# Seven-product pairs in four more projections of a hybrid decoder block, and a last column that keeps half of its weights

## The chip, the cores and the metric

The kernel runs on one core of one Trainium2 chip. The metric is the device time in microseconds (us) of one execution. Engines are named as in the profile: PE is TensorE's matmul, PEld its weight load, DVE is VectorE, ACT is ScalarE, POOL is GpSimd, SP is SyncE, which issues the weight DMAs.

## The reference

One layer of a decoder block over 256 tokens with a model width of 2048, in float32:

```python
u = rmsnorm(h, g_mix)
q, k, v, z, xbc, dt, g_a, g_s = split(u @ w_in)
out_a = sliding_window_attention(q, k, v) @ w_attn_br
y = rmsnorm(ssd(conv(xbc), dt) * silu(z), g_ssd)
out_s = y @ w_ssd_br
h = h + (sigmoid(g_a) * out_a + sigmoid(g_s) * out_s) @ w_o
f = rmsnorm(h, g_ffn)
h = h + (silu(f @ w_gate) * (f @ w_up)) @ w_down          # hidden width 5632
h = h + sigmoid(rmsnorm(h, g_ple) @ w_ple_gate) * (p @ w_ple_proj)
return rmsnorm(h, g_final)
```

## The kernel before

**Numbers in two parts.** Each float32 operand of a projection is split into a high part (a cast, on ACT) and a low part (the operand less its high part, on DVE). A product is three matmuls into one accumulator: high by high, high by low, low by high. The activations lie with features on partitions (uT, yT, mergedT, hT, actT, h2T: four k-tiles of 128 features by 256 tokens each, in both parts) and are the stationary operand, 128 tokens at a time; the weights are the moving operand, 512 columns at a time.

**`nblock`** computes one block of 512 columns for both token tiles. It loads two k-tiles of weights per step (512 KB, tile `wr`, a ring of 4), casts them (`wh`, a ring of 4), takes the low parts (`wl`, a ring of 3), issues 12 matmuls, and then runs one piece of side work. It uses two of the four PSUM tiles of one pool; transposes use the other pool.

**`wide_block`** (only in the hidden stage before) computes two blocks of 512 columns, those of `w_gate` and `w_up`, into four accumulators, and swaps the two PSUM pools each time. It goes by pairs of k-tiles. An ordinary pair is two loads of 512 KB and 24 matmuls. A seven-product pair takes a 2 x 2 block product (two token tiles, two k-tiles, two column blocks) in seven products, 21 matmuls, instead of eight: DVE makes four sums of weights (`tr`, split into `th` and `tl`), the activations come as four combinations (`forms`, made by `token_forms`), and four shared sums collect in the other pool's four PSUM tiles. After the last such pair the shared sums are combined into a large tile `mid` (`parts`). At the end of the block each accumulator is combined with its part. The hidden stage has such pairs at `hforms` 2 and 5, eight pairs to a block.

**Order.** The code is written in program order, and a scheduler orders the instructions of each engine from that order and from what each waits for, ahead of time; on the chip each engine takes its instructions in that order. `side` is a queue of pieces of work (transposes, normalization sums), one of which is run after each load's matmuls; `drain` runs what is left. `queue_flip` queues the two `transpose_pair`s by which 512 finished columns become features on partitions.

**Stages around the change**, with their times in the trace: the attention projection ends at about 500 us. Then come four columns, in turn the second gate (w_in at `GSO`, with uT) and the SSD projection (with yT), to 677 us; four columns of the output projection (with mergedT), to 769; and three thirds of the hidden width (4, 4 and 3 column blocks of `hidden`, each third followed by its part of the down projection over four columns, with actT), from 769 to 1490. Last comes the gate of the embedding: for each column `projected` and the gate product (with h2T). The weights of its last column are loaded and split ahead, two k-tiles a time (`load_last`), twice in each of the down columns 1 and 2 of the last third and of gate columns 1 and 2; the last column then runs from SBUF, token tile 0 first, then two halves of token tile 1, each followed by its finish. Large tiles (8 KB to a partition) share one pool of 17 buffers.

Of the kernel before, what the change touches and what calls it, by code (L numbers as in the profile page):

```python
# [11 lines left out]
F32 = mybir.dt.float32  # L12
# [49 lines left out]
def block_kernel(ctx: ExitStack, tc: tile.TileContext, x, x_t, p_t, positions, vecs, rows, g_final,  # L62
# [81 lines left out]
    def transpose_pair(src, col0, dst, j0, gains=None, form=None):  # L144

        ps = aux_tile().rearrange("p (j t) -> p j t", j=2)
        for j in range(2):
            for t in range(NT):
                c = col0 + j * P
                nc.tensor.transpose(out=ps[:, j, t * P:(t + 1) * P], in_=src[t][:, c:c + P],  # L150
                                    identity=ident)
        split_to(dst, j0, ps, gains)
        if form is not None:
            token_forms(ps, form, gains)
# [96 lines left out]
    def token_forms(src, dst, gains=None):  # L251


        sc = roll("fsc").rearrange("p (j t) -> p j t", j=2)
        for j in range(2):
            nc.scalar.activation(out=sc[:, j], in_=src[:, j], func=AF.Copy,
                                 scale=1.0 if gains is None else gains[j])
        fm = roll("fm").rearrange("p (f t) -> p f t", f=4)
        a11, a21, a12, a22 = sc[:, 0, :P], sc[:, 0, P:], sc[:, 1, :P], sc[:, 1, P:]
        for o, x, y, op in ((fm[:, 0], a22, a21, ALU.subtract), (fm[:, 1], fm[:, 0], a11, ALU.add),  # L260
                            (fm[:, 2], a12, fm[:, 1], ALU.subtract),
                            (fm[:, 3], a11, a21, ALU.subtract)):
            nc.vector.tensor_tensor(out=o, in0=x, in1=y, op=op)
        nc.scalar.copy(out=dst[:, :, 0], in_=fm)
        nc.vector.tensor_tensor(out=dst[:, :, 1], in0=fm, in1=dst[:, :, 0].bitcast(F32),
                                op=ALU.subtract)

    def wide_block(halves, lhs, nk, forms, pumps=1):
# [19 lines left out]
        for kp in range(np_):  # L288
# [56 lines left out]
        return [x.tile for x in sums], parts  # L345
# [277 lines left out]

    def hslice(g):
        return slice(g * HPG, (g + 1) * HPG)
# [37 lines left out]
    def queue_xs(g, src):  # L663
# [69 lines left out]
        def flip(i):  # L733
            def run():
                xd = mix[g, "xd"]
                transpose_pair([xd[:, t, 1] for t in range(NT)], i * 2 * P, yT[g], 2 * i,
                               [vcol(V_GSSD, 4 * g + 2 * i + j) for j in range(2)])
            return run
# [175 lines left out]
    mergedT = None  # L914
# [9 lines left out]
    drain(heads)  # L924
    r2 = const.tile([P, NT], F32, name="r2")
# [8 lines left out]
    mergedT = feat_tiles(4, "mergedT")  # L934

    def queue_flip(src, dst, j, gbase=None, forms={}):
        for i in range(2):
            def run(i=i):
                gains = None
# [5 lines left out]
    for j in range(4):  # L945
        accs = nblock(w_in, GSO + j * NB, lhs_u, KD)
        gs = [roll("gs") for _ in range(NT)]
        for t in range(NT):
            nc.scalar.activation(out=gs[t], in_=accs[0][t], func=AF.Sigmoid,
                                 scale=r1[:, t:t + 1])  # L950
        accs = nblock(w_ssd_br, j * NB, lambda k: stat(yT, k), KD)
        for t in range(NT):
            nc.vector.scalar_tensor_tensor(out=gs[t], in0=accs[0][t], scalar=r2[:, t:t + 1],
                                           in1=gs[t], op0=ALU.mult, op1=ALU.mult)
            nc.vector.tensor_tensor(out=merged[t][:, cols(j)], in0=merged[t][:, cols(j)],
                                    in1=gs[t], op=ALU.add)
        queue_flip(merged, mergedT, j)
# [6 lines left out]
    hT = feat_tiles(4, "hT")  # L964
    hforms = big([P, 2, 4, 2, P], F32R, name="hforms")
    hforms = {kp: hforms[:, i] for i, kp in enumerate((2, 5))}
# [6 lines left out]

    ssq3 = mean_parts(4, EPS, "ssq3")
    for j in range(4):
        accs = nblock(w_o, j * NB, lambda k: stat(mergedT, k), KD)
        for t in range(NT):
            nc.vector.tensor_tensor(out=h[t][:, cols(j)], in0=accs[0][t], in1=h[t][:, cols(j)],
                                    op=ALU.add)
        queue_flip(h, hT, j, V_GFFN, hforms)  # L980
        side.append(lambda j=j: square_sum(j, ssq3))
# [5 lines left out]
    def hidden(j, dst):  # L987
# [3 lines left out]
        for i, (o, op) in enumerate(((act[0], ALU.add), (parts[1], ALU.subtract),  # L991
                                     (act[1], ALU.add), (parts[3], ALU.subtract))):
            nc.vector.tensor_tensor(out=o, in0=sums[i], in1=parts[i], op=op)
# [5 lines left out]
        for i in range(2):  # L999
            side.append(lambda i=i: transpose_pair(act, i * 2 * P, dst, 2 * i))  # L1000

    last_h, last_l = [], []

    def load_last(c):


        if c % 2 == 0:
            last_h.append(big([P, 4, NB], F32R, name="last_h"))
            last_l.append(big([P, 4, NB], F32R, name="last_l"))
        wr = wraw_p.tile([P, 2, NB], F32, name="wr", tag="wr")  # L1010
        nc.sync.dma_start(out=wr, in_=w_ple_gate[c * 2 * P:(c + 1) * 2 * P, 3 * NB:].rearrange(
            "(k p) n -> p k n", p=P))
        ks = slice(2 * (c % 2), 2 * (c % 2) + 2)
        nc.scalar.copy(out=last_h[c // 2][:, ks], in_=wr)
        nc.vector.tensor_tensor(out=last_l[c // 2][:, ks], in0=wr,
                                in1=last_h[c // 2][:, ks].bitcast(F32), op=ALU.subtract)

    steps = deque(range(KD // 2))

    def run_ahead(chunks):  # L1020
        def run(c):
            if c in chunks and steps:
                load_last(steps.popleft())
        return run

    ssq4 = mean_parts(4, EPS, "ssq4")
    h2T = pT = gfin = None
    thirds = ((0, 4), (4, 8), (8, FFN // NB))
    for j0, j1 in thirds:
        last = j1 == FFN // NB  # L1030
        actT = []
        for j in range(j0, j1):
            actT.append(big([P, 2, 4, SEQ], F32R, name="actT"))
            hidden(j, actT[-1])
        drain()
        if last:
            h2T = feat_tiles(4, "h2T")
# [6 lines left out]
        for j in range(4):  # L1044
            accs = nblock(w_down[j0 * NB:j1 * NB], j * NB, lambda k, a=actT: stat(a, k),
                          4 * (j1 - j0), before=run_ahead((1, 3)) if last and j in (1, 2) else None)
            for t in range(NT):
                nc.vector.tensor_tensor(out=h[t][:, cols(j)], in0=accs[0][t],
                                        in1=h[t][:, cols(j)], op=ALU.add)
            if last:  # L1050
                queue_flip(h, h2T, j, V_GPLE)
                side.append(lambda j=j: square_sum(j, ssq4))
    drain()
    r4 = const.tile([P, NT], F32, name="r4")
# [4 lines left out]
    r5 = const.tile([P, NT], F32, name="r5")  # L1059
    def mix_in(t, ps, pp, c0, n):  # L1060
# [28 lines left out]
    def projected(j):  # L1089
        accs = nblock(w_ple_proj, j * NB, lambda k: stat(pT, k), PLE // P, tile_of=aux_tile)  # L1090
# [4 lines left out]

    nc.vector.memset(ssq5[:, :, 4:5], 0.0)
# [9 lines left out]
    for t in range(NT):  # L1106
        ts = slice(t * P, (t + 1) * P)
        for i, (s0, sn) in enumerate(((0, NB),) if t == 0 else ((0, NB // 2), (NB // 2, NB // 2))):
            o = acc_tile()[:, :sn]
            for k in range(KD):  # L1110
                hi, lo = stat(h2T, k)
                wh, wl = last_h[k // 4][:, k % 4], last_l[k // 4][:, k % 4]
                cs = slice(s0, s0 + sn)
                nc.tensor.matmul(o, hi[:, ts], wh[:, cs], start=(k == 0), stop=False)
                nc.tensor.matmul(o, hi[:, ts], wl[:, cs], start=False, stop=False)
                nc.tensor.matmul(o, lo[:, ts], wh[:, cs], start=False, stop=(k == KD - 1))
            mix_in(t, o, pp[t][:, cs], 3 * NB + s0, sn)
            square_in(t, 3 * NB + s0, sn, 3 + i)
            if s0 + sn < NB:
                gain_in(t, 3 * NB + s0, sn)  # L1120
        rsqrt_mean(ssq5[:, t:t + 1], r5[:, t:t + 1])
        gain_in(t, 3 * NB + s0, sn)
        finish(t)
# [57 lines left out]
```

## Time and profile before

| | us |
|---|---|
| median of 3 runs | 1599.76 |
| lowest, highest | 1598.59, 1599.88 |
| profiled execution, its time | 1600.46 |
| its span | 1598.8 |
| PE busy | 1584.0 (99%) |
| DVE busy | 1060.2 (66%) |
| ACT busy | 806.6 (50%) |

The span is that of the profiled execution, from the first to the last instruction; its time is 1.7 us longer than the span. Busy times of matmuls are of pipelined instructions: the mean of one 512-column matmul is about 390 ns long, and the next starts before it ends, so their pace is read from the starts.

### The profile page before, as it was taken

What the parts mean: (1) busy time and instruction counts of PE and PEld (TensorE: products, weight loads), DVE (VectorE), ACT (ScalarE), POOL (GpSimd) and SP (SyncE); (2) the same over time, 40 slices, a digit from 0 to 9 for tenths busy, and PEclk for the clock granted to TensorE, in tenths of its full rate; (3) what the DMA queues carried; (4) which work ended last, traced back from release to release, by engine and by line L of the source; (5) the groups of instructions that cost most, each with busy time, mean ns of one, the idle gap of its engine ahead of it and who ended that gap; (6) DMA issues with size and microseconds to landing.
All of it is one profiled execution on the core that took longest, in us unless ns stands there. A gap on an engine that the chain in (4) does not pass through costs nothing.

```text
span 1598.8 us, 19873 instructions
## 1 busy us (share of the span) xinstructions
PE 1584.0 (99%) x7348; PEld 1312.3 (82%) x7348; DVE 1060.2 (66%) x1274; ACT 806.6 (50%) x1020; POOL 131.6 (8%) x136
## 2 busy tenths in 40 slices
PE   9999999999999999999999999999999999999997
PEld 7988888888888888888888888888888888887886
DVE  7676767666655555456778775577775577776673
ACT  6654665555643444445554543445544344546552
POOL 1014224143210000000000000000000000000000
PEclk9999999999999999999999999999999999999999
DMA  8566435555657666655666656666665566756661
GB/s 267 172 193 186 143 105 158 158 160 157 178 185 218 190 190 185 197 184 185 185 192 203 194 189 197 187 204 194 194 196 188 193 187 204 225 194 223 198 211 53
DMA packets 152562, 296.63 MB, mean 186 GB/s; under 512 B 9537, under 2 KB 9665, under 8 KB 152081
## 3 DMA queue, kind: packets, MB, share of 16 engines
q1 hardware_dynamic: 151168, 290.76, 58.9%
q0 software_dynamic: 576, 3.47, 0.7%
q8 instruction: 57, 0.93, 0.2%
q10 hardware_dynamic: 720, 1.14, 0.2%
q14 instruction: 41, 0.33, 0.1%
HBM read 293.23 MB, written 2.10 MB: 185 GB/s over the span
## 4 chain that ended last, share of the span: by engine, by line
PE 94%; DMA 2%; ACT 1%; DVE 1%; issue 1%; POOL 0%; POOLq 0%; ACTq 0%; DVEq 0%; SPq 0%
PE acc L204 17%; PE acc L206 17%; PE acc L205 17%; PE aux L248 15%; PE acc L248 14%; PE aux L204 2%; PE aux L205 2%; PE aux L206 2%; PE aux L150 1%; DMA wr<-in_w_down_dram 1%; PE aux L709 1%; DVE wl L195 1%; PE aux L886 1%; PE acc L233 1%; PE aux L233 0%
## 5 line engine op out<-in xcount | busy, mean ns | idle before, releaser
L195 DVE TENSOR_TENSOR wl<-wr,wh 128x1024 fp32r<-128x1024 f32 (+1 forms) x356 | 452.3, 1274 | 324.3 <-PE acc L205 253.8
L193 ACT CAST wh<-wr 128x1024 fp32r<-128x1024 f32 (+1 forms) x356 | 367.6, 1035 | 439.7 <-PE acc L206 343.8
L204 PE MATMUL acc<-wh,uT 128*128 128x512 f32 (+1 forms) x640 | 250.6, 392 | 0.6 <-ACT cb L438 0.6
L206 PE MATMUL acc<-wh,uT 128*128 128x512 f32 (+1 forms) x640 | 243.9, 381 | 0.0
L205 PE MATMUL acc<-wl,uT 128*128 128x512 f32 (+1 forms) x640 | 243.6, 381 | 0.0
L298 DVE TENSOR_TENSOR wl<-wr,wh 128x1024 fp32r<-128x1024 f32 x132 | 159.4, 1221 | 61.8 <-issue 31.8
L248 PE MATMUL aux<-wh,hT 128*128 128x512 f32 x620 | 199.5, 391 | 0.0
L296 ACT CAST wh<-wr 128x1024 fp32r<-128x1024 f32 x132 | 138.6, 1054 | 115.9 <-PE aux L248 43.6
L248 PE MATMUL acc<-wh,hT 128*128 128x512 f32 x524 | 170.7, 392 | 0.0
L204 PEld LDWEIGHTS acc<-wh,uT 128*128 128x128 f32 x640 | 120.3, 188 | 22.8 <-issue 1.4
L206 PEld LDWEIGHTS acc<-wh,uT 128*128 128x128 f32 x640 | 120.1, 188 | 22.9
L205 PEld LDWEIGHTS acc<-wl,uT 128*128 128x128 f32 x640 | 120.4, 188 | 22.5 <-issue 1.0
L248 PEld LDWEIGHTS aux<-wh,hT 128*128 128x128 f32 x620 | 116.4, 188 | 24.0
L248 PE MATMUL aux<-wl,hT 128*128 128x512 f32 x310 | 120.7, 389 | 0.0
L248 PEld LDWEIGHTS acc<-wh,hT 128*128 128x128 f32 x524 | 98.4, 188 | 20.1
L248 PE MATMUL acc<-wl,hT 128*128 128x512 f32 x262 | 102.0, 389 | 0.0
L204 PE MATMUL acc<-wh,actT 128*128 128x512 f32 x256 | 99.8, 390 | 0.0
L206 PE MATMUL acc<-wh,actT 128*128 128x512 f32 x256 | 99.8, 390 | 0.0
L205 PE MATMUL acc<-wl,actT 128*128 128x512 f32 x256 | 99.6, 389 | 0.0
L324 ACT CAST wh<-wr 128x1024 fp32r<-128x1024 f32 (+1 forms) x44 | 36.9, 838 | 86.4 <-PE acc L248 43.1
L248 PEld LDWEIGHTS aux<-wl,hT 128*128 128x128 f32 x310 | 58.2, 188 | 11.7
L325 DVE TENSOR_TENSOR tl<-tr,th 128x2048 fp32r<-128x2048 f32 x22 | 50.4, 2290 | 11.6 <-ACT th L324 11.6
(344 smaller groups left out, 2572.8 us busy)
## 6 DMA issues: line engine op xcount, KB each, us to landing
wr<-in_w_in_dram SPq DMA_DIRECT2D x144, 512.0 KB, 3.6
wr<-in_w_gate_dram SPq DMA_DIRECT2D x88, 512.0 KB, 3.7
wr<-in_w_up_dram SPq DMA_DIRECT2D x88, 512.0 KB, 3.8
wr<-in_w_down_dram SPq DMA_DIRECT2D x88, 512.0 KB, 3.6
wr<-in_w_ssd_br_dram SPq DMA_DIRECT2D x32, 512.0 KB, 3.7
wr<-in_w_o_dram SPq DMA_DIRECT2D x32, 512.0 KB, 4.3
wr<-in_w_ple_gate_dram SPq DMA_DIRECT2D x32, 512.0 KB, 4.5
wr<-in_w_in_dram SPq DMA_DIRECT2D x32, 256.0 KB, 4.0
```

What stands on the lines that cost most here:

```text
L150: nc.tensor.transpose(out=ps[:, j, t * P:(t + 1) * P], in_=src[t][:, c:c + P], identity=ident)
L193: nc.scalar.copy(out=wh, in_=wr)
L195: nc.vector.tensor_tensor(out=wl, in0=wr, in1=wh.bitcast(F32), op=ALU.subtract)
L204: nc.tensor.matmul(o, hi[:, ts], wh[:, kk, cs], start=(k == 0), stop=False)
L205: nc.tensor.matmul(o, hi[:, ts], wl[:, kk, cs], start=False, stop=False)
L206: nc.tensor.matmul(o, lo[:, ts], wh[:, kk, cs], start=False, stop=(k == nk - 1))
L233: nc.tensor.matmul(o, hi[:, ts], wh[:, i], start=(k == 0), stop=False)
L248: nc.tensor.matmul(self.tile, a, b, start=self.first, stop=self.left == 0)
L296: nc.scalar.copy(out=wh, in_=wr)
L298: nc.vector.tensor_tensor(out=wl, in0=wr, in1=wh.bitcast(F32), op=ALU.subtract)
L324: nc.scalar.copy(out=xh, in_=x)
L325: nc.vector.tensor_tensor(out=xl, in0=x, in1=xh.bitcast(F32), op=ALU.subtract)
```

## The change

Four projections besides gate and up now go by `wide_block`, two column blocks of one weight matrix at a time (`column_pair`): the second gate with seven-product pairs 2 and 5 of eight (`uforms`, made from uT during the attention projection), the SSD projection with pair 4 (`yforms`), the output projection with pair 4 (`mforms`), and the down projection with pairs 2 and 5 of eight in the first two thirds and 3 of six in the last (`aforms`, made when the hidden columns are transposed). All of the second gate is computed ahead of the SSD projection, and its two wide blocks of gates are kept. Each accumulator is combined with its part by `settle` or, where it is added to h, by `add_settled`, two instructions. The large tiles of transposed activations are allocated when they are first written. The last column of the embedding's gate keeps only the second half of its k-tiles ahead (four loads, two of them in gate column 2 and two in the last column itself); the first half is loaded, split and used step by step for the three output pieces together, and then the kept half is run piece by piece, each followed by its finish.

```diff
-    def token_forms(src, dst, gains=None):
+    def scaled(ps, gains=None):
         sc = roll("fsc").rearrange("p (j t) -> p j t", j=2)
         for j in range(2):
-            nc.scalar.activation(out=sc[:, j], in_=src[:, j], func=AF.Copy,
+            nc.scalar.activation(out=sc[:, j], in_=ps[:, j], func=AF.Copy,
                                  scale=1.0 if gains is None else gains[j])
+        return sc
+
+    def joined(tiles, kp):
+        ks = slice(2 * (kp % 2), 2 * (kp % 2) + 2)
+        sc = roll("fsc").rearrange("p (j t) -> p j t", j=2)
+        src = tiles[kp // 2].bitcast(F32)
+        nc.vector.tensor_tensor(out=sc, in0=src[:, 0, ks], in1=src[:, 1, ks], op=ALU.add)
+        return sc
+
+    def token_forms(sc, dst):
...
+    def settle(i, sums, parts, out=None):
+        nc.vector.tensor_tensor(out=parts[i] if out is None else out, in0=sums[i], in1=parts[i],
+                                op=ALU.subtract if i % 2 else ALU.add)
+
+    def add_settled(i, dst, sums, parts):
+        nc.vector.tensor_tensor(out=dst, in0=dst, in1=parts[i],
+                                op=ALU.subtract if i % 2 else ALU.add)
+        nc.vector.tensor_tensor(out=dst, in0=sums[i], in1=dst, op=ALU.add)
...
+    YPAIRS, yforms = (4,), {}
...
+    UPAIRS = (2, 5)
...
+    side.extend(u_forms(kp) for kp in UPAIRS)
...
-    mergedT = feat_tiles(4, "mergedT")
+    mergedT = []
...
-    for j in range(4):
-        accs = nblock(w_in, GSO + j * NB, lhs_u, KD)
-        gs = [roll("gs") for _ in range(NT)]
...
-        accs = nblock(w_ssd_br, j * NB, lambda k: stat(yT, k), KD)
...
-        queue_flip(merged, mergedT, j)
+    gates = []
+    for jj in range(2):
+        sums, parts = wide_block(column_pair(w_in, GSO, jj), lhs_u, KD, uforms)
+        for i in range(4):
+            settle(i, sums, parts)
+            nc.scalar.activation(out=parts[i], in_=parts[i], func=AF.Sigmoid,
+                                 scale=r1[:, i // 2:i // 2 + 1])
+        gates.append(parts)
+    mforms = form_tiles((4,), "mforms")
+    for jj in range(2):
+        sums, parts = wide_block(column_pair(w_ssd_br, 0, jj), lambda k: stat(yT, k), KD, yforms)
+        for i in range(4):
+            t, c = i // 2, cols(2 * jj + i % 2)
+            settle(i, sums, parts)
+            nc.vector.scalar_tensor_tensor(out=parts[i], in0=parts[i], scalar=r2[:, t:t + 1],
+                                           in1=gates[jj][i], op0=ALU.mult, op1=ALU.mult)
+            nc.vector.tensor_tensor(out=merged[t][:, c], in0=merged[t][:, c], in1=parts[i],
+                                    op=ALU.add)
+        for q in range(2):
+            queue_flip(merged, mergedT, 2 * jj + q, None, mforms)
...
-        accs = nblock(w_o, j * NB, lambda k: stat(mergedT, k), KD)
...
+        add_to_h(jj, *wide_block(column_pair(w_o, 0, jj), lambda k: stat(mergedT, k), KD, mforms))
...
-    thirds = ((0, 4), (4, 8), (8, FFN // NB))
+    thirds = ((0, 4, (2, 5)), (4, 8, (2, 5)), (8, FFN // NB, (3,)))
...
-            accs = nblock(w_down[j0 * NB:j1 * NB], j * NB, lambda k, a=actT: stat(a, k),
-                          4 * (j1 - j0), before=run_ahead((1, 3)) if last and j in (1, 2) else None)
...
+            add_to_h(jj, *wide_block(column_pair(w_down[j0 * NB:j1 * NB], 0, jj),
+                                     lambda k, a=actT: stat(a, k), 4 * (j1 - j0), aforms))
...
-                      before=run_ahead((1, 4)) if j else None)
+                      before=run_ahead((3, 6)) if j == 2 else None)
...
+    ahead = run_ahead((0, 2))
+    for c in range(KD // 4):
+        ahead(c)
+        wr = wraw_p.tile([P, 2, NB], F32, name="wr", tag="wr")
+        nc.sync.dma_start(out=wr, in_=w_ple_gate[2 * c * P:2 * (c + 1) * P, 3 * NB:].rearrange(
+            "(k p) n -> p k n", p=P))
...
+        for kk in range(2):
+            for piece in range(3):
+                step(piece, 2 * c + kk, wh[:, kk], wl[:, kk])
+    for piece, (t, c0, n) in enumerate(pieces):
+        for i in range(KD // 2):
+            kh, kl = kept[i // 4]
+            step(piece, KD // 2 + i, kh[:, i % 4], kl[:, i % 4])
+        mix_in(t, outs[piece], pp[t][:, c0:c0 + n], 3 * NB + c0, n)
...
```

## Rows read from the trace of the kernel before

**Rows 1.** The page: span, and each engine's busy us, share of the span and instructions.

```profile
span 1598.8 us, 19873 instructions
...
PE 1584.0 (99%) x7348; PEld 1312.3 (82%) x7348; DVE 1060.2 (66%) x1274; ACT 806.6 (50%) x1020; POOL 131.6 (8%) x136
```

**Rows 2.** Windows by stage: us, busy us of each engine, granted clock, DMA share, GB/s.

```profile
547.00:591.50 44.50, 44.50 (x203) 36.85 (x201) 23.52 (x23) 19.10 (x20) 0.00 (x0) 1.00 0.62 189
...
812.00:855.50 43.50, 43.50 (x196) 35.60 (x195) 34.88 (x40) 23.20 (x25) 0.00 (x0) 1.00 0.64 194
1419.50:1489.70 70.20, 69.44 (x321) 56.95 (x320) 46.48 (x54) 39.06 (x56) 0.00 (x0) 1.00 0.64 210
1516.00:1541.00 25.00, 25.00 (x112) 20.71 (x111) 18.45 (x20) 15.42 (x20) 0.00 (x0) 1.00 0.73 236
1566.90:1590.00 23.10, 22.82 (x146) 20.66 (x145) 8.08 (x15) 5.25 (x12) 0.92 (x1) 1.00 0.13 46
```

**Rows 3.** The chain of waits in order of time: start us, length us, what.

```profile
547.01 0.44 PE aux L150 x4
...
591.48 0.44 PE aux L150 x4
...
703.23 0.44 PE aux L150 x4
...
725.94 0.44 PE aux L150 x4
...
812.08 2.72 PE acc L248 x12
...
843.92 11.56 PE acc L248 x51
855.48 2.72 PE aux L248 x12
```

**Rows 4.** Groups of DVE, first third of hidden blocks: count, busy us, mean ns.

```profile
L298 DVE TENSOR_TENSOR wl<-wr,wh 128x1024 fp32r<-128x1024 f32 x46 | 55.4, 1221 | 21.4 <-issue 11.9 <-PE aux L248 7.3 <-PE acc L248 2.2
...
L325 DVE TENSOR_TENSOR tl<-tr,th 128x2048 fp32r<-128x2048 f32 x8 | 18.3, 2290 | 3.5 <-ACT th L324 3.5
...
L316 DVE TENSOR_TENSOR tr<-wr 128x512 f32<-128x512 f32 x16 | 10.6, 686 | 0.5 <-DMA wr<-in_w_up_dram 0.5
...
L325 DVE TENSOR_TENSOR wl<-wr,wh 128x512 fp32r<-128x512 f32 x8 | 5.5, 689 | 1.9 <-PE aux L248 1.1 <-PE acc L248 0.7
L343 DVE TENSOR_TENSOR mid<-mid,aux 128x512 f32<-128x512 f32 x8 | 5.3, 684 | 0.1
...
L996 DVE SCALAR_TENSOR_TENSOR act<-mid,r,act 128x512 f32<-128x512 f32 x6 | 4.2, 745 | 0.0
```

**Rows 5.** Groups of DVE, output projection and start of the hidden stage.

```profile
L978 DVE TENSOR_TENSOR h<-acc,h 128x512 f32<-128x512 f32 x8 | 5.5, 688 | 3.9 <-PE acc L206 3.9
...
L265 DVE TENSOR_TENSOR hforms<-fm,hforms 128x512 fp32r<-128x512 f32 x2 | 1.4, 687 | 0.0
...
L263 DVE TENSOR_TENSOR fm<-fsc 128x128 f32<-128x128 f32 x4 | 1.0, 285 | 0.0
```

**Rows 6.** Timeline of DVE at the end of a hidden block, which is at 855.48.

```profile
852.12 0.69 DVE L993 TENSOR_TENSOR act<-acc,mid 128x512 f32<-128x512 f32 x1 [0.98 <-PE acc L248]
852.73 1.22 DVE L298 TENSOR_TENSOR wl<-wr,wh 128x1024 fp32r<-128x1024 f32 x1
...
855.45 1.22 DVE L298 TENSOR_TENSOR wl<-wr,wh 128x1024 fp32r<-128x1024 f32 x1
```

**Rows 7.** Waits of the weight loads, first third of hidden blocks.

```profile
PEld aux L248 <- DVE tl L325: 0.7, 2, 0.4
...
PEld acc L248 <- DVE tl L325: 0.4, 1, 0.4
```

**Rows 8.** The chain of waits at the end, token tile 0.

```profile
1578.24 0.70 ACT gt L1064
...
1581.41 0.92 POOL r L176
```

More of the change, by code (lines that the diff above doesn't have):

```diff
@@ L153, in transpose_pair @@
         if form is not None:
[L154 removed]
+            token_forms(scaled(ps, gains), form)
     def feat_tiles(n, name):
@@ L345, in wide_block, with form_tiles, column_pair @@
         return [x.tile for x in sums], parts
+    def settle(i, sums, parts, out=None):
[5 more added lines that the diff above has]
+        nc.vector.tensor_tensor(out=dst, in0=sums[i], in1=dst, op=ALU.add)
+    def form_tiles(pairs, name):
+        tile = big([P, 2, 4, 2, P], F32R, name=name)
+        return {kp: tile[:, i] for i, kp in enumerate(pairs)}
+    def column_pair(w, col0, jj):
+        return tuple((w, col0 + (2 * jj + q) * NB) for q in range(2))
     warm = roll("warm")
@@ L924, in block_kernel, with u_forms, run @@
     drain(heads)
+    UPAIRS = (2, 5)
+    uforms = {}
+    def u_forms(kp):
+        def run():
+            if kp == UPAIRS[0]:
+                uforms.update(form_tiles(UPAIRS, "uforms"))
+            token_forms(joined(uT, kp), uforms[kp])
+        return run
+    side.extend(u_forms(kp) for kp in UPAIRS)
     r2 = const.tile([P, NT], F32, name="r2")
@@ L972, in square_sum, with add_to_h @@
                                  accum_out=ssq[:, t, j:j + 1])
+    def add_to_h(jj, sums, parts):
+        for i in range(4):
+            add_settled(i, h[i // 2][:, cols(2 * jj + i % 2)], sums, parts)
     ssq3 = mean_parts(4, EPS, "ssq3")
-    for j in range(4):
-        accs = nblock(w_o, j * NB, lambda k: stat(mergedT, k), KD)
[L977 to L981, printed above, removed]
+    for jj in range(2):
+        add_to_h(jj, *wide_block(column_pair(w_o, 0, jj), lambda k: stat(mergedT, k), KD, mforms))
+        for q in range(2):
+            queue_flip(h, hT, 2 * jj + q, V_GFFN, hforms)
+            side.append(lambda j=2 * jj + q: square_sum(j, ssq3))
     drain()
@@ L984, in block_kernel, with hidden @@
     rsqrt_mean(ssq3, r3)
-    def hidden(j, dst):
+    def hidden(j, dst, kp0, forms):
         sums, parts = wide_block(((w_gate, j * NB), (w_up, j * NB)), lambda k: stat(hT, k), KD,
@@ L990, in hidden @@
         act = [roll("act") for _ in range(NT)]
-        for i, (o, op) in enumerate(((act[0], ALU.add), (parts[1], ALU.subtract),
-                                     (act[1], ALU.add), (parts[3], ALU.subtract))):
-            nc.vector.tensor_tensor(out=o, in0=sums[i], in1=parts[i], op=op)
+        for i in range(4):
+            settle(i, sums, parts, None if i % 2 else act[i // 2])
         for t in range(NT):
@@ L999, in hidden @@
         for i in range(2):
[L1000 to L1024, printed above, removed]
+            side.append(lambda i=i: transpose_pair(act, i * 2 * P, dst, 2 * i, None,
+                                                   forms.get(kp0 + i)))
     ssq4 = mean_parts(4, EPS, "ssq4")
-    h2T = pT = gfin = None
-    thirds = ((0, 4), (4, 8), (8, FFN // NB))
-    for j0, j1 in thirds:
+    h2T, pT, gfin = [], None, None
+    thirds = ((0, 4, (2, 5)), (4, 8, (2, 5)), (8, FFN // NB, (3,)))
+    for j0, j1, apairs in thirds:
         last = j1 == FFN // NB
         actT = []
+        aforms = form_tiles(apairs, "aforms")
         for j in range(j0, j1):
             actT.append(big([P, 2, 4, SEQ], F32R, name="actT"))
-            hidden(j, actT[-1])
+            hidden(j, actT[-1], 2 * (j - j0), aforms)
         drain()
         if last:
-            h2T = feat_tiles(4, "h2T")
             pT = [big([P, 2, 2, SEQ], F32R, name="pT")]
@@ L1094, in projected, with keep, run_ahead, run @@
         return pp
+    kept = []
+    def keep(c):
+        if c % 2 == 0:
+            kept.append([big([P, 4, NB], F32R, name="kept") for _ in range(2)])
+        kh, kl = kept[c // 2]
+        wr = wraw_p.tile([P, 2, NB], F32, name="wr", tag="wr")
+        k0 = KD // 2 + 2 * c
+        nc.sync.dma_start(out=wr, in_=w_ple_gate[k0 * P:(k0 + 2) * P, 3 * NB:].rearrange(
+            "(k p) n -> p k n", p=P))
+        ks = slice(2 * (c % 2), 2 * (c % 2) + 2)
+        nc.scalar.copy(out=kh[:, ks], in_=wr)
+        nc.vector.tensor_tensor(out=kl[:, ks], in0=wr, in1=kh[:, ks].bitcast(F32),
+                                op=ALU.subtract)
+    steps = deque(range(KD // 4))
+    def run_ahead(chunks):
+        def run(c):
+            if c in chunks and steps:
+                keep(steps.popleft())
+        return run
     nc.vector.memset(ssq5[:, :, 4:5], 0.0)
@@ L1105, in block_kernel @@
     pp = projected(3)
[L1106 to L1123, printed above, removed]
+    pieces = ((0, 0, NB), (1, 0, NB // 2), (1, NB // 2, NB // 2))
@@ new lines, in block_kernel, with step @@
+    outs = [tile_of()[:, :n] for tile_of, (_, _, n) in zip((acc_tile, acc_tile, aux_tile), pieces)]
+    def step(piece, k, wh, wl):
+        t, c0, n = pieces[piece]
+        hi, lo = stat(h2T, k)
+        ts, cs = slice(t * P, (t + 1) * P), slice(c0, c0 + n)
+        nc.tensor.matmul(outs[piece], hi[:, ts], wh[:, cs], start=(k == 0), stop=False)
+        nc.tensor.matmul(outs[piece], hi[:, ts], wl[:, cs], start=False, stop=False)
+        nc.tensor.matmul(outs[piece], lo[:, ts], wh[:, cs], start=False, stop=(k == KD - 1))
```

49 lines of the change are left out of this document (29 added, 20 removed).

## The prediction

> **What bounds the kernel now.** I read the page first. TensorE is busy for 99% of a span of 1598.8 us, VectorE for 66%, ScalarE for 50% [rows 1]. A busy TensorE need not be one at its limit, so I looked for the pace next, in the chain of waits in order of time: 51 matmuls of 512 columns take 11.56 us there [rows 3], 0.2267 us each. The granted clock is 1.00 in every stage [rows 2], the 2.4 GHz level, and the 51 follow each other without a gap, so what fills the span is matmuls at one pace. Third, the windows by stage: the excess of each stage over its matmuls. One column of gate plus SSD projection is 192 matmuls and 8 transposes (0.11 us each: four are a piece of 0.44 us), 43.52 + 0.88 = 44.40 us; its period is 591.48 - 547.01 = 44.47 [rows 3]. One column of the output projection is 21.76 + 0.88 = 22.64; its period is 725.94 - 703.23 = 22.71 [rows 3]. So the old blocks lose 0.07 us each. A wide block of the hidden stage, which already has two seven-product pairs, is 186 matmuls and 8 transposes, 42.16 + 0.88 = 43.04; its period is 855.48 - 812.08 = 43.40 [rows 3]: it loses 0.36 us, 0.18 per such pair. It does so with VectorE busy for 34.88 of 43.5 us [rows 2]. Only matmuls that vanish, or waits that appear, move the time.
>
> **Matmuls removed.** An ordinary pair of k-tiles over two column blocks takes 8 products of 3 matmuls; a seven-product pair takes 7. New pairs: second gate, 2 blocks with 2 pairs; SSD projection, 2 with 1; output projection, 2 with 1; down projection, 2 x (2 + 2 + 1). That is 4 + 2 + 2 + 10 = 18 pairs, 54 matmuls, 54 x 0.2267 = 12.24 us off TensorE. Nothing is added there: transposes and the last block's matmuls stay, so TensorE's count goes from 7348 to 7294. The Trainium skill (TensorE: Matmul & The Clock Gate, Back-to-back issue gap) gives 131 ns per 512-column matmul in a sustained stream of loads and matmuls, and 215.7 ns for the isolated gap; by the first the 54 would be worth 7.1 us, an estimate. This trace does not agree with 131 ns: it shows 226.7.
>
> **What VectorE gets.** One seven-product pair costs it four adds at 0.686, a split of 1024 at 1.22, one of 512 at 0.689 and one of 2048 at 2.290 [rows 4], 6.95 us, against 2 x 1.22 = 2.44 before: +4.5, times 18 = 81 us. Each of 12 new wide blocks adds four shared sums at 0.684 [rows 4], 33 us. Settling costs 16 x 0.69 = 11 us in gate and SSD; the output and down projections do 64 adds in place of 32, +22 us at 0.688 [rows 5]. Nine form builds (two for u, one for y, one for merged, five for act) cost 4 x 0.285 + 0.687 = 1.83 us each [rows 5], 16.5, and the two u joins 1.4. In all some 165 us: VectorE goes from 1060 to about 1225 us, 77%.
>
> **Does that hide?** Per wide block, VectorE against TensorE: gate 12 x 1.22 + 2 x 6.95 + 2.74 + 2.75 = 34.0 of 42.2 us; SSD 17.1 + 6.95 + 2.74 + 2.75 + 4 x 0.745 + 4 x 0.688 = 35.3, and 38 where flips are pumped, of 42.8 + 0.9; output 17.1 + 6.95 + 2.74 + 5.5 + flips and forms 5.7 = 38 of 43.7; down 36.8 of 42.2. The hidden stage runs at 34.88 of 43.4, so on average all of it hides behind TensorE, and the nearest row prices it: 0.18 us a pair, 3.2 us for 18, less 8 x 0.07 that the old gate/SSD and output blocks lost: +2.7 us. Of the tl waits of the hidden stage [rows 7] there is 1.1 us over eight pairs, the same order. Bounds: nothing, and 12 x 0.36 x 2 = 8.6 us if each block loses twice what a hidden one does.
>
> **Bursts at block ends.** A low-part buffer ring of three lets VectorE be two loads (5.4 us of matmuls) ahead when a block ends; then the block's evacuation is queued ahead of the next low parts. In the hidden stage that is four settles and two multiplies, 4.2 us, and the timeline shows low parts slipping in between, where the next settle still waits for its sum [rows 6]. The output and down blocks leave four settles at the end (their first adds need only shared sums and h, ready earlier), 2.8 us: no more than hidden. The SSD block is the one that is worse: settle, scale and add for four tiles, 12 instructions, 8.5 us. Its first two sums end 3.4 and 2.7 us ahead of the block's end, so about 5.5 us lie behind the end, plus a low part of 1.22: late by 1.3 us if all twelve go first, not late if one low part slips in. I take 0.5 between the two SSD blocks and 1.0 into the output projection, where four flips (2.8 us) are drained too. Output into hidden (four flips of 2 x 0.48, one form) and down into the last gate: 0.4 each. Together +2.3; bounds 0 and 8.
>
> **Forms of the activations.** Two of four hidden blocks now build forms: +1.83 us VectorE in 43.4, 84% busy. Cover: the matmuls of that block. +0.5; bounds 0 and 5 x 1.83 = 9.2.
>
> **Down projection, last third.** Now 70.2 us for 288 matmuls and 32 transposes, 65.3 + 3.5 = 68.8 [rows 2]: 1.4 us is lost where four extra loads with their splits lie among 24. They move away; I take half back: -0.7 (0 to -1.4).
>
> **Last gate blocks.** Extra loads leave down and gate column 1; column 2 has two, as before, where 236 GB/s ran without a gap [rows 2]. The last column now loads six times 512 KB in the first half of its 22.8 us [rows 2]: 3.1 MB in 11.4 us, 276 GB/s, with one load of the embedding projection just ahead. SP issues these through the ring of four, so a held kept load holds the streamed ones behind it. +0.7; bounds 0 and 3 (six loads at the 236 GB/s of column 2 take 13.3 us, +1.9, and a start-up). At the end token tile 0 now finishes with half the column, about 5.7 us ahead of TensorE's end instead of 11.4; from its sigmoid to its root is 4.1 us [rows 8], so it just fits; sharing ScalarE and VectorE with the next piece: +0.3 (0 to 1.5).
>
> **Sum.** -12.24 - 0.7 + 2.7 + 2.3 + 0.5 + 0.7 + 0.3 = -6.4 us. The profiled execution took 1600.46, so 1594.0; it lies 0.7 above the median of 1599.76, so I predict **1593.3 us**.
>
> **Rivals.**
> *Everything hides.* Only -12.24 - 1.4 count, and half the pair price: 1586.5 to 1590. For it: hidden blocks lose only 0.36 us at 80% VectorE. Against: no row shows twelve evacuations in a row. Chance 0.22.
> *Bursts eat the gain.* SSD and drained boundaries at 6 to 8 us in place of 2.3, or forms at 3: 1597 to 1601. For: boundary work has priority over low parts. Against: the slipping in [rows 6]. Chance 0.14.
> *VectorE falls behind inside the pairs (slower).* A pair wants 6.95 us of VectorE in 21 x 0.2267 = 4.76 us, 2.2 us short, and lives off look-ahead. Where buffers are full (17 large ones; up to 17 tiles alive in gate and hidden blocks) the sums of weights come late, and the pair stalls. With the gain of 6.4 spread over 18 pairs, 0.36 us more per pair brings it to nothing; from 0.53 on it is slower by over 0.2%, and at the full 2.2 us it is 1593.3 + 36 = 1629. Against: hidden pairs have the same look-ahead, 22 times over. Chance 0.08.
> *TensorE is not the bound, and removed matmuls return as waits.* 1599.8. Against: the pace of 0.2267 with no gaps. Chance 0.04. The Trainium skill (Perfetto Trace Analysis, Identifying the Most-Contended Engine) says that matmul busy time is a bad measure of headroom and weight-load busy a good one; that is 82% here, which would speak for this rival. The trace does not bear it out: one weight load per matmul is 0.188 of 0.2267 us, 83%, so a stream without a gap shows just that.
>
> **Numbers.** The forecast, 1590 to 1597, has 0.52. About 0.2%, 3.2 us, can be told from no change. Faster than 1596.6: 0.49 of the forecast, 0.22, and 0.02 of the bursts, 0.73. Within: 0.03 + 0.12 + 0.04 = 0.19. Slower: 0.08. Range 1587.0 to 1600.5: it leaves out the slower rival, the lower edge of the first and little more.
>
> **What would show it.** TensorE with 7294 matmuls at 0.227 us; VectorE near 1225 us. Periods of wide blocks: gate about 42.5, SSD and output 43.7 to 45, down 42.5 in the first two thirds. Wrong if low parts or tl hold TensorE for microseconds behind SSD blocks, if form pairs gap more than 0.4 us, or if the last column waits for its loads.

## The result, and the profile after

The changed kernel takes 1613.89 us (median of four runs, 1613.52 to 1615.62), the kernel before 1599.17 (four runs too, 1598.09 to 1599.88). The ratio is 1.0095 with an interval of 1.0082 to 1.0107: 14.7 us slower, where 6.4 us faster was forecast and the range ended at 1600.5. The profiled execution took 1613.52, its span is 1611.8.

The page of the kernel after, to be read beside [rows 1]:

```profile
span 1611.8 us, 19994 instructions
...
PE 1578.9 (98%) x7294; PEld 1305.7 (81%) x7294; DVE 1202.3 (75%) x1507; ACT 845.7 (52%) x1073; POOL 130.3 (8%) x136
```

The 54 matmuls are gone, as forecast, and VectorE has 1202 us (forecast 1225). TensorE's busy time fell by 5 us while the span grew by 13: TensorE idles where it did not before, and some of the matmuls left are longer. The waits of the matmuls say where (engine, tile, line, releaser: us in total, times, longest; left out are waits of stages ahead of the change, 2.3 us in two of the new pairs, and 0.6 in the last column):

```profile
PE aux L150 <- DVE act L1049: 5.0, 2, 2.5
PE acc L150 <- DVE act L1049: 2.5, 1, 2.5
PE acc L204 <- DVE flipT L139: 2.5, 1, 2.5
PE aux L150 <- DVE merged L1007: 2.5, 2, 2.1
...
PE aux L248 <- DVE flipT L139: 1.5, 1, 1.5
...
PE aux L248 <- ACT fsc L255: 1.0, 1, 1.0
PE aux L150 <- DVE h L366: 0.7, 1, 0.7
```

These seven rows are 15.7 us. L150 is the transpose in `transpose_pair`; L248 and L204 are the first matmuls of a block, waiting for the evacuation of transposes (`flipT`, `fsc`). None is released by a weight or by a sum of weights. The timeline puts them at six places, all of them ends of stages (start, duration, engine, line, what, and in brackets the idle time before it with its releaser):

```profile
673.59 0.44 PE L150 MATMUL aux<-ident,merged 128*128 128x128 f32 x2 [0.38 <-DVE merged L1007]
676.11 1.97 PE L150 MATMUL aux<-ident,merged 128*128 128x128 f32 x8 [2.09 <-DVE merged L1007]
679.10 0.80 PE L248 MATMUL aux<-wh,flipT 128*128 128x512 f32 x1 [1.02 <-ACT fsc L255]
...
771.46 0.88 PE L150 MATMUL aux<-ident,h 128*128 128x128 f32 x6 [0.74 <-DVE h L366]
772.61 0.69 DVE L328 TENSOR_TENSOR tr<-wr 128x512 f32<-128x512 f32 x1 [0.43 <-DMA wr<-in_w_up_dram]
773.85 0.47 PE L248 MATMUL aux<-wh,flipT 128*128 128x512 f32 x1 [1.51 <-DVE flipT L139]
...
947.54 0.39 PE L248 MATMUL acc<-wh,flipT 128*128 128x512 f32 x1
947.90 1.22 DVE L310 TENSOR_TENSOR wl<-wr,wh 128x1024 fp32r<-128x1024 f32 x1
949.03 0.68 DVE L360 TENSOR_TENSOR mid<-acc,mid 128x512 f32<-128x512 f32 x1
949.63 1.41 DVE L1049 SCALAR_TENSOR_TENSOR act<-mid,r,act 128x512 f32<-128x512 f32 x2
950.43 0.44 PE L150 MATMUL aux<-ident,act 128*128 128x128 f32 x2 [2.50 <-DVE act L1049]
950.62 0.48 PE L248 MATMUL aux<-wh,actT 128*128 128x512 f32 x1
951.70 0.59 ACT L132 CAST actT<-aux 128x512 fp32r<-128x512 f32 x1 [2.64 <-PE aux L150]
...
1498.12 1.91 PE L150 MATMUL acc<-ident,h 128*128 128x128 f32 x16
1502.51 0.47 PE L204 MATMUL acc<-wh,pT 128*128 128x512 f32 x1 [2.49 <-DVE flipT L139]
```

Read the tile names. At 950.43 a transpose writes a tile of the pool `aux`, and the first matmul of the down projection behind it, at 950.62, writes the same pool. The transpose needs `act` and starts 2.9 us after the start of the hidden block's last matmul: VectorE has a low part, a settle and two products to do there. The down projection's first matmul waits for nothing of its own; it goes 0.19 us after the transpose, and before the transposes are evacuated (from 951.70). So for this matmul the pool has a free tile; only the order holds it. At 679.10, 773.85 and 1502.51, where a whole queue of transposes stood ahead, the first matmul of the stage waits until they are evacuated as well. Ahead of 773.85 VectorE makes a sum of weights between two evacuations (772.61) and has waited 0.43 us for its DMA; with the pools in order, below, it does the same (at 765.55, behind 0.41 us) and TensorE does not wait. The other two hidden thirds end like the one at 950.43, at 1212.38 and 1429.57, each with 2.50 us. Each time transposes and the next accumulators share a pool: `aux` at 679, 773, 950 and 1212, `acc` at 1429 and 1502.

Why that is so can be read from the code; the scheduler's choice itself is in no trace, and the experiments test it. The new `wide_block` swaps the two PSUM pools at its start. The transposes that `drain` runs after a stage's last block take the pool of the shared sums, and the swap then makes just that pool the one of the next block's accumulators (before the embedding's gate, an explicit `psum.reverse()` does so). The tiles of a pool are handed out in the order of the code. In the kernel before, `nblock` took its accumulators from the pool that the transposes did not use, so that the down and output projections could start past them; only the first block of a hidden third came behind a swap.

The waits are not all. A piece of the chain of waits of the kernel after (start, length, what), at the start of the second gate and of the hidden stage:

```profile
499.58 10.88 PE aux L248 x48
...
773.85 12.78 PE aux L248 x48
```

The same 48 matmuls take 1.90 us more behind a stall. The windows of the kernel after (us, busy time of PE, PEld, DVE, ACT, POOL, granted clock, DMA share, GB/s) show why:

```profile
951.00:964.00 13.00, 13.00 (x62) 10.81 (x61) 10.61 (x13) 6.83 (x8) 0.00 (x0) 1.00 0.42 136
679.00:692.00 13.00, 12.90 (x53) 10.52 (x54) 8.51 (x14) 4.71 (x7) 0.00 (x0) 0.87 0.38 121
773.80:786.80 13.00, 12.95 (x50) 10.56 (x51) 10.68 (x18) 8.98 (x18) 1.08 (x1) 0.87 0.34 97
1429.70:1443.00 13.30, 13.30 (x56) 11.03 (x57) 8.11 (x11) 4.86 (x6) 0.00 (x0) 0.87 0.36 115
```

The granted clock is 0.87 behind three of the six stalls, a mean over stretches at the 2.4 and at the 1.2 GHz level; the windows of [rows 2] had 1.00. The Trainium skill (TensorE: Matmul & The Clock Gate, A second HAM failure mode: psum-queue depth-cycling) tells of another kernel, in which frequent short idles of TensorE between groups of matmuls made the clock fall and rise, and the throughput paid for it. The trace agrees that the clock can fall behind a short idle and that it costs, here 1.90 us.

**Theory A**, then, is the PSUM pool: drained transposes stand ahead of the next accumulators, and TensorE waits with them for VectorE: for what they transpose and, where a whole queue stands ahead, for their evacuation too. **Rival B** is that VectorE itself is the cause: seven-product pairs and twelve evacuations make it late at the block ends, and another pool would only move the wait.

### The profile page after: what moved, and what is told of

Same layout as the page of the kernel before. It is cut to its first block, busy times and chain, and to the rows that moved or that the text cites. A ratio compares the mean times of both kernels' runs of the same rounds, so it can differ in the third digit from the quotient of the medians.

```text
span 1611.8 us, 19994 instructions
## 1 busy us (share of the span) xinstructions
PE 1578.9 (98%) x7294; PEld 1305.7 (81%) x7294; DVE 1202.3 (75%) x1507; ACT 845.7 (52%) x1073; POOL 130.3 (8%) x136
## 4 chain that ended last, share of the span: by engine, by line
PE 94%; DVE 2%; ACT 2%; DMA 1%; issue 1%; POOL 0%; POOLq 0%; DVEq 0%; ACTq 0%
PE aux L248 30%; PE acc L248 28%; PE acc L204 9%; PE acc L205 9%; PE acc L206 9%; PE aux L150 1%; DMA wr<-in_w_ple_gate_dram 1%; PE aux L739 1%; PE aux L920 1%; PE acc L233 1%; PE acc L235 0%; PE acc L234 0%; PE aux L233 0%; PE aux L678 0%; PE aux L234 0%
## 5 line engine op out<-in xcount | busy, mean ns | idle before, releaser
L308 ACT CAST wh<-wr 128x1024 fp32r<-128x1024 f32 x280 | 294.0, 1054 | 285.2 <-PE aux L248 109.4
L310 DVE TENSOR_TENSOR wl<-wr,wh 128x1024 fp32r<-128x1024 f32 x280 | 338.8, 1221 | 83.2 <-PE aux L248 27.7
L195 DVE TENSOR_TENSOR wl<-wr,wh 128x1024 fp32r<-128x1024 f32 (+1 forms) x172 | 227.3, 1328 | 126.8 <-PE acc L205 96.9
L193 ACT CAST wh<-wr 128x1024 fp32r<-128x1024 f32 (+1 forms) x172 | 173.8, 1014 | 175.0 <-PE acc L206 136.6
L248 PE MATMUL aux<-wh,flipT 128*128 128x512 f32 x736 | 238.0, 394 | 2.5 <-DVE flipT L139 1.5
L248 PE MATMUL acc<-wh,flipT 128*128 128x512 f32 x640 | 208.3, 392 | 0.0
L204 PE MATMUL acc<-wh,uT 128*128 128x512 f32 (+1 forms) x512 | 200.2, 391 | 0.7 <-ACT cb L466 0.7
L205 PE MATMUL acc<-wl,uT 128*128 128x512 f32 (+1 forms) x512 | 193.8, 379 | 0.0
L248 PEld LDWEIGHTS aux<-wh,flipT 128*128 128x128 f32 x736 | 139.3, 189 | 32.3 <-issue 2.0
L248 PE MATMUL aux<-wl,flipT 128*128 128x512 f32 x368 | 144.3, 392 | 0.0
L248 PEld LDWEIGHTS acc<-wh,flipT 128*128 128x128 f32 x640 | 120.2, 188 | 24.5
L336 ACT CAST wh<-wr 128x1024 fp32r<-128x1024 f32 x80 | 66.9, 837 | 122.0 <-PE acc L248 62.3
L248 PE MATMUL acc<-wl,flipT 128*128 128x512 f32 x320 | 124.6, 389 | 0.0
L204 PEld LDWEIGHTS acc<-wh,uT 128*128 128x128 f32 x512 | 96.3, 188 | 18.2 <-issue 1.4
L205 PEld LDWEIGHTS acc<-wl,uT 128*128 128x128 f32 x512 | 96.3, 188 | 17.6 <-issue 1.0
L248 PE MATMUL aux<-wh,actT 128*128 128x512 f32 x292 | 94.4, 392 | 0.0
L248 PE MATMUL acc<-wh,actT 128*128 128x512 f32 x292 | 93.7, 392 | 0.0
```

The costliest lines, as they stand in the source:

```text
L193: nc.scalar.copy(out=wh, in_=wr)
L195: nc.vector.tensor_tensor(out=wl, in0=wr, in1=wh.bitcast(F32), op=ALU.subtract)
L204: nc.tensor.matmul(o, hi[:, ts], wh[:, kk, cs], start=(k == 0), stop=False)
L205: nc.tensor.matmul(o, hi[:, ts], wl[:, kk, cs], start=False, stop=False)
L248: nc.tensor.matmul(self.tile, a, b, start=self.first, stop=self.left == 0)
L308: nc.scalar.copy(out=wh, in_=wr)
```

## The experiments

Every ratio is to the kernel before, run beside it on the same chip (medians 1599.06 to 1599.36), with a 95% interval.

**The swap moved to the end of the block.** The only edit to the changed kernel is where the pools are swapped, so that drained transposes and the next accumulators have different pools.

```diff
 def wide_block(...):
-        psum.reverse()
...
+        psum.reverse()
         return [x.tile for x in sums], parts
...
     gates = []
+    psum.reverse()
...
     drain()
-    psum.reverse()
```

> Theory A (PSUM pools): at the end of a stage the drained transposes take their PSUM tiles from the very pool from which the next wide block takes its four accumulators, so its first matmuls stand behind the transposes and their evacuation. Here the two pools are swapped at the end of each wide block instead of at the start of the next, so that drained transposes get the pool of the sums just settled. The idle stretches of TensorE at six stage ends (4.5 us into the output projection, 2.6 into hidden, 2.7 into each of three down projections, 2.7 into the last gate, some 18 us) and about 3 us at the half clock behind them go, and one or two ordinary waits come back: 1592 to 1597. Theory B (VectorE's bursts at block ends and the work in the pairs hold TensorE): VectorE's work is the same, the time stays at 1610 or more.

Measured: 1589.55 us (1588.25 to 1591.93), ratio 0.9939 [0.9925, 0.9954]. It is 24.3 us below the changed kernel's median, 9.5 below the kernel before, and below the 1592 to 1597 that A gave. The page and the waits of this kernel:

```profile
span 1586.8 us, 19976 instructions
...
PE 1571.6 (99%) x7294; PEld 1301.1 (82%) x7294; DVE 1200.1 (76%) x1507; ACT 844.4 (53%) x1073; POOL 131.5 (8%) x136
```

```profile
PE aux L248 <- DVE wl L336: 0.7, 1, 0.7
...
PE acc L248 <- DVE wl L336: 0.3, 1, 0.3
```

VectorE has the same work, 1200 us, and the seven waits are gone; what is left in wide blocks is these two, 1.0 us. The timeline of TensorE at the start of the output projection, where the changed kernel stood still for three waits:

```profile
672.47 0.39 PE L248 MATMUL acc<-wh,yT 128*128 128x512 f32 x1
672.70 0.39 PE L248 MATMUL aux<-wh,flipT 128*128 128x512 f32 x1
...
673.38 0.38 PE L150 MATMUL acc<-ident,merged 128*128 128x128 f32 x2
673.52 0.48 PE L248 MATMUL aux<-wh,flipT 128*128 128x512 f32 x1
```

The stage goes on 0.23 us after the last matmul of the one before, and the transposes, now in `acc`, come in between. A holds, B falls for this change. The first 512-column matmul of each stage in the timelines, us:

| | before | after | swap at the end | after less swap at the end |
|---|---|---|---|---|
| second gate | 500.60 | 499.42 | 499.65 | -0.2 |
| output projection | 677.54 | 679.10 | 672.70 | 6.4 |
| first hidden third | 768.94 | 773.85 | 763.32 | 10.5 |
| its down projection | 942.11 | 950.62 | 937.10 | 13.5 |
| second down projection | 1202.41 | 1212.57 | 1195.39 | 17.2 |
| third down projection | 1419.70 | 1429.76 | 1409.75 | 20.0 |
| embedding gate | 1489.95 | 1502.51 | 1477.55 | 25.0 |
| last column | 1567.16 | 1578.76 | 1554.59 | 24.2 |
| end of the span | 1598.8 | 1611.8 | 1586.8 | 25.0 |

The lag grows across each stretch that holds a stalled stage end, and otherwise only in the last column, by 0.8. Of the 25.0 us, 15.7 are the seven waits; 1.3 is that the two pairs that wait for `wl` in the second gate and the first down projection do so for 1.2 and 1.1 us in the changed kernel in place of 0.7 and 0.3; 0.6 is a wait for a low part in the last column, which the other kernel does not have. That is 17.6 us of idle time, and the two pages agree: the span less PE's busy time is 32.9 us in the changed kernel and 15.2 with the swap at the end, 17.7 less. The other 7.3 us are a longer busy time of the same 7294 matmuls. Three stretches at 0.87 at about 1.9 each, by the one that was measured, would be 5.7 of them; the rest was not taken apart.

**The same fault put into the kernel before.** No block of it is changed; the pools are swapped around the down projections, so that their accumulators share the pool of the drained transposes.

```diff
         drain()
+        psum.reverse()
...
             if last:
                 queue_flip(h, h2T, j, V_GPLE)
                 side.append(lambda j=j: square_sum(j, ssq4))
+        psum.reverse()
     drain()
```

> The kernel before, with one thing changed: at the end of each third of the hidden width the pools are swapped after the drain, so that the down projection's accumulators come from the pool that the drained transposes use. No seven-product pair and no VectorE work is added. Theory A: TensorE stands about 2.7 us at each of three stage ends, 1605 to 1609. Theory B: no change, 1598 to 1601.

Measured: 1609.84, ratio 1.0064 [1.0048, 1.0081]: 10.8 us lost with not one pair added, just over the upper end that A gave. The timeline of TensorE at the first of the three places:

```profile
940.45 0.39 PE L248 MATMUL acc<-wh,hT 128*128 128x512 f32 x1
943.34 0.44 PE L150 MATMUL aux<-ident,act 128*128 128x128 f32 x2 [2.50 <-DVE act L996]
943.53 0.48 PE L204 MATMUL aux<-wh,actT 128*128 128x512 f32 x1
```

It is the row of the changed kernel to the hundredth: 2.89 us from start to start, 2.66 more than between two neighbouring matmuls. Three times that is 8.0; the rest, 2.8, fits PE's busy time, 1586.9 us in place of 1584.0 for the same matmuls: the clock fell behind two of the three stalls (last section).

**The same pool, but the accumulators first.** Is it sharing or order that costs? Here the kernel before has one pool for both during the down projections, and the `drain` is left out, so that the transposes come as side work behind the first load's matmuls.

```diff
-        drain()
+        pools = list(psum)
+        psum[:] = [pools[1], pools[1]]
...
                 side.append(lambda j=j: square_sum(j, ssq4))
+        psum[:] = pools
     drain()
```

> As e2_before_same_pool, accumulators and transposes of the down projections share one pool, but the last transposes of each third are not drained ahead of the down projection: they stay queued and follow its first load, so that in program order the accumulators are handed their PSUM tiles first. If it is the order in which one pool's tiles are handed out that holds the accumulators back, the three waits of 2.66 us go: 1598 to 1601. If sharing the pool is what costs, they stay: 1607 to 1610.

Measured: 1599.63, ratio 1.0001 [0.9992, 1.0011]. The timeline of TensorE at the first start of a down projection:

```profile
941.53 0.39 PE L248 MATMUL acc<-wh,hT 128*128 128x512 f32 x1
941.75 0.39 PE L204 MATMUL aux<-wh,actT 128*128 128x512 f32 x1
```

No gap. Here the transposes stand behind matmuls in the code, and so they are handed their tiles behind them. The kernel before has them ahead in the code, but in the other pool, and no gap either (its down projection starts 0.22 us after the hidden block's last matmul, at 942.11). So neither sharing a pool nor standing behind a transpose costs by itself; the two together do.

**One stage end alone.** The kernel with the swap at its end gets the fault back in one place, behind the SSD blocks.

```diff
             queue_flip(merged, mergedT, 2 * jj + q, None, mforms)
+    psum.reverse()
     drain()
+    psum.reverse()
```

> As e1_pool, but at the one stage end between the SSD and the output projection the pools are swapped back around the drain, so that its four pairs of transposes take the pool of the next accumulators again. Theory A: TensorE's idle stretches come back at this one place, 4.5 us, with 1 to 3 us at the half clock behind them: 5 to 8 us over e1_pool, near 1596. If the changed kernel's 24 us came from the pools' being swapped elsewhere (inside blocks), there is no more than 1 us.

Measured: 1597.09, ratio 0.9986 [0.9977, 0.9995], 7.5 us more than without (1589.55; the kernels before, each run beside its own, differ by 0.2). Its timeline there:

```profile
673.24 0.44 PE L150 MATMUL aux<-ident,merged 128*128 128x128 f32 x2 [0.38 <-DVE merged L1008]
675.77 1.09 PE L150 MATMUL aux<-ident,merged 128*128 128x128 f32 x8 [2.09 <-DVE merged L1008]
678.41 0.79 PE L248 MATMUL aux<-wh,flipT 128*128 128x512 f32 x1 [1.55 <-ACT fsc L255]
```

The three waits are those of the changed kernel, two of them to the hundredth. They make 4.0 us; the rest is mostly behind them, where the granted clock is 0.80:

```profile
679.00:692.00 13.00, 13.00 (x50) 10.47 (x49) 7.31 (x12) 4.42 (x6) 0.00 (x0) 0.80 0.37 120
```

This one stage end eats most of what all eighteen pairs bring.

**The order right, but no new pairs.** The kernel with the swap at its end does the four projections by ordinary pairs: no forms are built, settling is a copy, and adding to h one instruction. All else of the change stays.

```diff
-    YPAIRS, yforms = (4,), {}
+    YPAIRS, yforms = (None,), {}
...
-    side.extend(u_forms(kp) for kp in UPAIRS)
...
-    mforms = form_tiles((4,), "mforms")
+    mforms = {}
...
-        aforms = form_tiles(apairs, "aforms")
+        aforms = {}
```

> As e1_pool, but the four projections' wide blocks have ordinary pairs only, and their forms are not built: 54 matmuls more, some 130 us less of VectorE. If the pairs keep most of what they remove (12.2 us less 0.18 us each), it is 8 to 10 us slower than e1_pool, near 1603. If the pairs hold TensorE as much as they save (theory B), it is no slower than e1_pool.

Measured: 1599.05, ratio 0.9997 [0.9988, 1.0007]. So the eighteen pairs are worth 1599.05 - 1589.55 = 9.5 us, as expected (8 to 10; the 1603 beside it reckoned with a slower kernel to start from). That is 0.53 each of the 0.68 that three matmuls take; the interval of the first ratio alone leaves 7.4 to 12.0 us in all. Everything else in the change together is worth nothing that can be measured.

**More pairs.** If B is wrong here, does VectorE have room for more? Four kernels add pairs to the one with the swap at its end: two in each output block (2 and 5 for 4), two in each SSD block (4 and 6), two in each down block of the last third (2 and 4 for 3), and all three at once.

```diff
-    YPAIRS, yforms = (4,), {}
+    YPAIRS, yforms = (4, 6), {}
...
-    mforms = form_tiles((4,), "mforms")
+    mforms = form_tiles((2, 5), "mforms")
...
-    thirds = ((0, 4, (2, 5)), (4, 8, (2, 5)), (8, FFN // NB, (3,)))
+    thirds = ((0, 4, (2, 5)), (4, 8, (2, 5)), (8, FFN // NB, (2, 4)))
```

All three:

> As e1_pool, with a second seven-product pair in the SSD blocks (pair 6), in the output blocks (2 and 5) and in the last third of the down projection (2 and 4): 6 pairs, 18 matmuls, 4.1 us less on TensorE, 4.5 us more VectorE each. At the 0.53 us that a pair kept between e3 and e1 it is 3.2 us under e1_pool, near 1586.4. If VectorE, now 90% of an SSD block, holds TensorE, it is no faster than e1_pool.

The output blocks alone:

> As e1_pool, with two seven-product pairs (2 and 5) in place of one (4) in the two blocks of the output projection, and nothing else of e6_more_pairs. Two pairs more, 1.4 us of matmuls less. In the trace of e6 the output projection lost most. If pair 2 comes too soon behind the SSD blocks' 12 evacuations and transposes for VectorE, it is 3 to 8 us slower than e1_pool; if only the sum of e6's three edits was too much, it is 1 us faster.

The SSD blocks alone:

> As e1_pool, with pairs 4 and 6 in place of pair 4 alone in the two SSD blocks, and nothing else of e6. If a late pair puts its VectorE work (6.95 us, and the shared sums) on top of the evacuations at the block's end, the output projection's start gaps and it is 3 to 8 us slower than e1_pool; else 1 us faster.

The last third alone:

> As e1_pool, with pairs 2 and 4 in place of pair 3 in the two blocks of the last third of the down projection, and nothing else of e6. If the late pair does the same there, into the last gate, it is 3 to 10 us slower than e1_pool; else 1 us faster.

| | us | ratio to before | against 1589.55 |
|---|---|---|---|
| all three | 1608.19 | 1.0051 [1.0034, 1.0068] | +18.6 |
| output | 1594.18 | 0.9968 [0.9958, 0.9977] | +4.6 |
| SSD | 1595.40 | 0.9974 [0.9965, 0.9983] | +5.9 |
| last third | 1600.73 | 1.0008 [0.9999, 1.0018] | +11.2 |

The last three take 6 matmuls away each, 1.4 us, and the first 18; all are slower than 1589.55, the last third by more than the 3 to 10 us expected. (The kernel before was 0.2 to 0.3 us slower beside these than beside 1589.55.) For the SSD blocks the timeline shows it, VectorE first, then TensorE:

```profile
670.06 1.23 DVE L309 TENSOR_TENSOR wl<-wr,wh 128x1024 fp32r<-128x1024 f32 x1 [3.96 <-ACT wh L307]
671.20 2.79 DVE L354 TENSOR_TENSOR mid<-mid,aux 128x512 f32<-128x512 f32 x4
673.91 0.69 DVE L360 TENSOR_TENSOR mid<-acc,mid 128x512 f32<-128x512 f32 x1
...
676.91 0.69 DVE L1008 TENSOR_TENSOR merged<-merged,mid 128x512 f32<-128x512 f32 x1
...
671.61 0.39 PE L248 MATMUL acc<-wh,yT 128*128 128x512 f32 x1
...
672.29 0.39 PE L248 MATMUL aux<-wh,flipT 128*128 128x512 f32 x1
677.65 0.69 PE L150 MATMUL acc<-ident,merged 128*128 128x128 f32 x2 [4.97 <-DVE merged L1008]
```

The last pair is now one pair from the block's end. VectorE stands for 3.96 us at a low part whose cast is late, and the four combinations of the shared sums (2.79 us) are queued behind it. The settle at 673.91 starts 2.3 us behind the block's last matmul (671.61); without the added pair, the same settle starts at 671.90, 0.6 us ahead of that matmul (672.47). So `merged` is late. The pools are in order here: the transposes write `acc`, and TensorE has already issued three matmuls of the next stage, which write `aux`. But the scheduler set the transposes next, and TensorE does not go past them. The Trainium skill (PSUM — Partial Sum Buffer, Engine vs sequencer instructions) says that matmuls start in program order; the trace agrees, with this wait of 4.97 us. With the output pairs the waits are for casts and low parts inside blocks, 3.5 us. With those of the last third they are the same (L248), and `h` and low parts in the gate behind it (L150, L205); the largest:

```profile
PE acc L205 <- DVE wl L195: 2.5, 2, 1.7
...
PE aux L248 <- DVE wl L309: 1.7, 2, 1.0
...
PE aux L150 <- DVE h L366: 1.4, 2, 1.1
PE aux L248 <- ACT wh L307: 1.3, 1, 1.3
```

These are 6.9 of its 11.2 + 1.4 us. By the pages the idle time of TensorE is 3.3 us (output), 6.2 (SSD) and 9.2 (last third) above that of the kernel without the added pair, and its busy time 1.6, 2.2 and 2.8 above, with 6 matmuls fewer; that second part was not taken apart. Rival B, which does not explain the change, is real one step further on. The fastest version that was run is the changed kernel with the swap at the end of the block.

## Why the prediction was wrong

**The matmuls removed** were right in count, 7294. Of their 12.24 us the prediction's prices leave 12.24 - 18 x 0.18 - 0.5 for the forms = 8.5; the pairs brought 9.5 once the pools were in order.

**What VectorE gets, and whether it hides**: right in the main. 1202 us against 1225, and the two waits inside wide blocks are 2.3 us in the changed kernel and 1.0 with the swap at the end. The prediction's sign of being wrong, a gap of over 0.4 us in a pair, holds for two of eighteen pairs in the first and for one in the second. With the swap at the end the first column pair of the second gate takes 43.2 us (499.81 to 543.00 in the chain), the second 42.2 (543.00 to 585.16); about 42.5 was forecast.

**Bursts at block ends** is the step that failed. It gave +2.3 with bounds of 0 and 8, and it was the transition from one stage to the next that it got wrong: "1.0 into the output projection", "Output into hidden (...) and down into the last gate: 0.4 each", and nothing for hidden into down. With the clock behind them, these are what the moved swap gives back, 24.3 us, but for the 2 us of idle time in the two pairs and the last column. The step counted what VectorE has to do behind a block's end and compared it with the look-ahead of the low parts, as if TensorE could always run that look-ahead off. It could not: its next matmuls had no accumulator before the transposes of the last block had theirs. The prediction tells of `drain`ed flips as VectorE's work alone, and never asked which pool they write and which pool the next block takes, though the diff shows `wide_block`, and with it the swap, go from one stage to five. With the pools in order the same step is worth little, as far as is known: without pairs, the rest of the change is at 1599.05, where the prediction's other terms (-0.56 - 0.7 + 2.3 + 0.7 + 0.3) make 2.0 us more than before; the interval leaves from 1.9 us less to 1.1 more.

**The last column**: +1.0 forecast. From its first matmul to the end of the span (the table's last two rows) it is 31.6 us before, 33.0 after, 0.6 of it the wait for a low part, and 32.2 with the swap at the end. The size was right.

**The rivals.** "Bursts eat the gain" had the right place, the drained stage ends, with 6 to 8 us as its price and VectorE's priority as its cause; both were wrong. "VectorE falls behind inside the pairs" had the right sign and the wrong mechanism. The kernel with the swap at the end, 1589.55, lies just below the forecast's 1590 to 1597, in the range of "everything hides" (1586.5 to 1590).

## What to carry to other kernels

Where two uses of PSUM take turns in two pools, write down for every stage end which pool the last side work takes and which one the next accumulators take: a transpose that waits for an evacuation, handed its tile first, holds up all matmuls behind it, ready or not. A change that moves a swap, or gives a helper that swaps to more stages, changes this order without touching a single duration, and the place of one swap can decide the sign of a gain. And when a change takes work off the busiest engine and the time rises, read the waits by their place first: here 15.7 us stood at stage ends and 2.3 in the new pairs.

## What the runs showed of the hardware

The same idle time does not always cost the same. In the changed kernel the three stalls at the hidden thirds' ends have the same 2.50 us, and the granted clock behind them is 1.00, 1.00 and 0.87 (13 us from 951.0, 1212.5 and 1429.7). In the kernel before with the fault it is 1.00 behind the first and 0.87 behind the second and third; two of its windows:

```profile
943.50:957.00 13.50, 13.50 (x65) 11.19 (x65) 6.63 (x7) 5.30 (x6) 0.00 (x0) 1.00 0.47 154
1206.50:1220.00 13.50, 13.21 (x55) 10.98 (x56) 5.90 (x7) 4.34 (x5) 0.00 (x0) 0.87 0.37 119
```

The second window holds ten matmuls and transposes fewer than the first, 0.3 us of it idle. So a stall of 2.5 us costs 2.66 us alone, and more where the clock falls behind it: about 1.9 by the hidden stage, 1.4 by what is left of the 10.8 us for two. Which of the two comes was not to be foreseen from its length.
